# A hybrid GLA and Fourier layer on one core: folding the Fourier input before its projection instead of after it

## The chip, the core and the metric

The kernel runs on one core of one Trainium2 chip. Five engines work from queues of their own, each strictly in the order in which its instructions were written: TensorE (PE in the profile, with its weight loads shown apart as PEld), VectorE (DVE), ScalarE (ACT), GpSimd (POOL) and SyncE (SP), which issues the transfers between main memory and the on-chip memory. An instruction also waits for semaphores that other engines and landed transfers raise. The metric is the device time of one launch in microseconds (us), the median of several runs. Nothing is loaded ahead of the launch: all weights, some 360 MB of 32-bit floats, are read once in every run.

## What is computed

One layer of a backbone is applied to 128 context positions and 256 latent positions of width 2048 (384 rows in all). A modulated, normalised input `h` goes through one combined projection, whose last 1024 columns are four Fourier groups of 256 channels. The change is in this branch:

```python
proj = h @ lw['w_in']
q, k, v, g, lr_f, lr_b, fo = jnp.split(proj, splits, axis=-1)
...
fg = fo.astype(jnp.float32).reshape(bsz, t, FOURIER_GROUPS, FOURIER_GROUP_DIM)
f = jnp.fft.fft2(fg, axes=(1, 3), norm='ortho').real
f = f.reshape(bsz, t, FOURIER_WIDTH).astype(h.dtype)
gates = jax.nn.sigmoid(h @ lw['w_gate'] + lw['b_gate'])
g_a, g_b = jnp.split(gates, 2, axis=-1)
merged = g_a * (o @ lw['w_br_gla']) + g_b * (f @ lw['w_br_four'])
return merged @ lw['w_out'], s_f, s_b
```

The transform is taken over positions and over the channels of a group, apart for context (128 positions) and latent (256 positions). Only its real part is kept. The real part of such a product is cos times cos minus sin times sin; a cosine sum needs only the even part of its input (x[n] plus x[N-n]) and a sine sum only the odd part (x[n] minus x[N-n]). So half of the input, folded, is enough for each. Around this branch stand a gated linear attention (GLA) with two scans, a modulation computed from a large weight (`w_ada`), an output projection, and a feed-forward part that fills the second half of the run.

## The kernel before, in words

**Number format.** Each weight tile and each activation is split into a high part (the value rounded to the fast 32-bit matmul format, made by a ScalarE copy) and a low part (the rest, made by a VectorE subtraction). A product is the sum of three matmuls: high times high, high times low, low times high.

**The weight stream.** Weights come through one queue of tiles of 128 x 1024 floats (512 KB). `load()` (L193) issues the transfer of the next tile into one of two buffers named `raw`. `split()` (L214) makes its high part `whi` (L227) and its low part `wlo` (L228), four buffers each. `push()` is one load and one split; `take()` gives the oldest split tile to the matmuls; `grab()` (L248) does both. Three split tiles stand ready ahead of the one in use. A third tile's transfer can be issued only when the first tile's buffer has been read for the last time, which is its low-part subtraction.

**Stages.** After a head stage (up to some 130 us) come six q and k tiles and then 32 gate tiles (`proj`, L281), each of two weight tiles with 24 matmuls of 384 columns. During the gates a side generator advances the GLA by a step per weight tile, and a second generator, `ada_rest` (L589), advances the modulation: one step loads one more 512 KB tile `adaw` and runs two VectorE multiply-adds over 1024 elements (L600). `rate[0]` is the number of such steps per turn: 1.0 in the gates, 0.9 in the Fourier stage, 0 in the mixing stage, 0.82 in the output projection.

**The Fourier stage** (L991 to L1027). The 384 rows of `h` are the stationary operand and 512 columns of the weight the moving one: for each half of the channels, eight weight tiles of 18 matmuls (`products`, L266, called for the tile `pfo`). Then VectorE forms the channel sums and differences `ed` (L1009 to L1011). The generator `dft` transforms first over positions (`left`, L914, with tables `cd`) and then over channels (`turn_channels`, L950, with tables `cs2` and `odd`), in plain 32-bit matmuls (`pp`, `pn`, `pe`), into `eT` and `dT`. The channel N/2 (`nyq`) is handled apart. Half of this lies in the Fourier stage, half in the first steps of the next.

**The mixing stage** (L1083 to L1107). `mix_order` (L160) interleaves three kinds of work: 8 output gate tiles ("o": two weight tiles each, evicted by `gcol`), 16 Fourier branch tiles ("b", `four`, L1054; the weight is folded over its channels by `fold`, L204, into a tile `ws`), and 16 GLA branch tiles ("a"). Of the 16 "b", ten stand among the "o" and six among the "a".

The order on PE, DVE, ACT and POOL is exactly that of the program text. On SP the transfers are placed by the framework, near the place where they are called, and are issued in that order.

## Time and profile before

| what | value |
|---|---|
| median of 3 runs | 1953.94 us (1952.92 to 1954.0) |
| span of the profiled execution | 1950.6 us |
| PE busy | 1936.3 us (99%), 10422 matmul records |
| DVE busy | 1633.1 us (84%) |
| ACT busy | 906.9 us (46%) |
| DMA | 380.12 MB, mean 195 GB/s |
| chain that ended last | PE 96%, DVE 2%, DMA 2%, ACT 1% |

The span is the time from the first to the last instruction of one profiled execution. The median lies some 3.3 us above it, for what lies around the program. PE records overlap one another (the next matmul starts while the last drains), so the duration of one record is longer than the distance from one matmul to the next, and it is the distance that counts. A plain 32-bit matmul shows two records.

### The profile page before, as it was taken

The page shows a single profiled execution, that of the slowest core. Times are in us where ns is not written, and L with a number is a line of the kernel's source. Part 1 is how long each engine was busy: PE and PEld are TensorE (multiplying, and loading weights), DVE is VectorE, ACT ScalarE, POOL GpSimd, SP SyncE. Part 2 cuts the span into 40 slices and gives each one's busy share as a digit, 9 for nine tenths or more (in the row PEclk, how much of TensorE's full clock was granted, in tenths as well). Part 3 has the DMA queues.
Part 4 walks back from the last instruction along what each step waited for, and adds up shares of the span by engine and source line. Part 5 has one row for each costly group of instructions (what it writes and reads, how often), then busy time and mean ns, then how long its engine had stood idle before and what let it go on. Part 6 is the DMA issues. An engine that isn't in the chain of part 4 may idle for free.

```text
span 1950.6 us, 27243 instructions
## 1 busy us (share of the span) xinstructions
PE 1936.3 (99%) x10422; PEld 1705.2 (87%) x10422; DVE 1633.1 (84%) x2114; ACT 906.9 (46%) x1270; POOL 33.6 (2%) x55
## 2 busy tenths in 40 slices
PE   9999999999999999999999999999999999999998
PEld 5779999999889999999988888888888888888886
DVE  5668888878777797977789898999898999887876
ACT  4233554544336654446454444444444444444444
POOL 0000000000000000004000000000000000000001
PEclk9999999999999999999999999999999999999999
DMA  9978677767765786655355535463636263626244
GB/s 391 382 255 272 228 257 239 231 218 244 239 198 178 236 265 212 233 188 210 93 157 162 172 125 179 137 199 112 199 120 209 93 216 98 211 75 194 67 157 144
DMA packets 201179, 380.12 MB, mean 195 GB/s; under 512 B 14160, under 2 KB 127508, under 8 KB 196696
## 3 DMA queue, kind: packets, MB, share of 16 engines
q1 hardware_dynamic: 200520, 378.12, 58.4%
q8 instruction: 82, 1.34, 0.3%
q14 instruction: 49, 0.40, 0.1%
q10 hardware_dynamic: 528, 0.26, 0.0%
HBM read 361.55 MB, written 16.78 MB: 194 GB/s over the span
## 4 chain that ended last, share of the span: by engine, by line
PE 96%; DVE 2%; DMA 2%; ACT 1%; issue 0%; SPq 0%; POOL 0%; DVEq 0%; ACTq 0%; POOLq 0%
PE pmm L261 32%; PE pgu L273 30%; PE pdn L273 18%; PE pfo L273 3%; PE pv L415 3%; PE pgm L398 1%; PE pf L1064 1%; PE pmm L1320 1%; DMA slab<-in_w_ada 1%; PE ptr L1612 1%; PE pf L1065 1%; PE po L673 1%; DMA xraw<-in_w_x 0%; PE px L433 0%; DMA raw<-in_w_d 0%; DVE x1b L1764 0%
## 5 line engine op out<-in xcount | busy, mean ns | idle before, releaser
L261 PE MATMUL pmm<-A_hi,whi 128*128 128x384 f32 x1072 | 361.3, 337 | 0.0
L261 PE MATMUL pmm<-A_hi,wlo 128*128 128x384 f32 x1072 | 358.6, 335 | 0.0
L261 PE MATMUL pmm<-A_lo,whi 128*128 128x384 f32 x1072 | 358.5, 334 | 0.0
L1467 ACT CAST whi<-u 128x1024 fp32r<-128x1024 f32 x200 | 210.6, 1053 | 271.0 <-DVE u L1451 86.2
L227 ACT CAST whi<-raw 128x1024 fp32r<-128x1024 f32 x181 | 189.5, 1050 | 208.1 <-DMA raw<-in_w_gate 69.0
L1467 ACT CAST whi<-raw 128x1024 fp32r<-128x1024 f32 x175 | 184.2, 1053 | 212.1 <-DMA raw<-in_w_g 68.0
L228 DVE TENSOR_TENSOR wlo<-raw,whi 128x1024 fp32r<-128x1024 f32 x179 | 218.1, 1221 | 66.2 <-ACT whi L227 65.5
L1478 DVE TENSOR_TENSOR wlo<-u,whi 128x1024 fp32r<-128x1024 f32 x200 | 243.9, 1220 | 28.1 <-ACT whi L1467 16.9
L273 PE MATMUL pgu<-whi,A_hi 128*128 128x512 f32 x640 | 250.0, 391 | 0.0
L273 PE MATMUL pgu<-whi,A_lo 128*128 128x512 f32 x640 | 249.3, 389 | 0.0
L1478 DVE TENSOR_TENSOR wlo<-raw,whi 128x1024 fp32r<-128x1024 f32 x175 | 213.3, 1219 | 33.9 <-ACT whi L1467 24.6
L600 DVE SCALAR_TENSOR_TENSOR adacc<-adaw,spad,adacc 128x1024 f32<-128x1024 f32 x180 | 222.8, 1279 | 0.3
L261 PEld LDWEIGHTS pmm<-A_hi,whi 128*128 128x128 f32 x1072 | 201.2, 188 | 3.0 <-issue 1.4
L261 PEld LDWEIGHTS pmm<-A_lo,whi 128*128 128x128 f32 x1072 | 201.3, 188 | 0.3
L261 PEld LDWEIGHTS pmm<-A_hi,wlo 128*128 128x128 f32 x1072 | 201.2, 188 | 0.0
L273 PE MATMUL pdn<-whi,hid_hi 128*128 128x512 f32 x480 | 186.9, 389 | 0.0
L273 PE MATMUL pdn<-whi,hid_lo 128*128 128x512 f32 x480 | 186.8, 389 | 0.0
L273 PE MATMUL pgu<-wlo,A_hi 128*128 128x512 f32 x640 | 184.2, 389 | 0.0
L273 PEld LDWEIGHTS pgu<-whi,A_hi 128*128 128x128 f32 x640 | 120.1, 188 | 26.0 <-issue 0.8
L273 PEld LDWEIGHTS pgu<-wlo,A_hi 128*128 128x128 f32 x640 | 120.1, 188 | 25.4
L273 PEld LDWEIGHTS pgu<-whi,A_lo 128*128 128x128 f32 x640 | 120.1, 188 | 25.0
L273 PE MATMUL pgu<-whi,S 128*128 128x512 f32 x480 | 131.1, 395 | 0.0
(386 smaller groups left out, 2900.0 us busy)
## 6 DMA issues: line engine op xcount, KB each, us to landing
adaw<-in_w_ada SPq DMA_DIRECT2D x96, 512.0 KB, 4.1
raw<-in_w_d SPq DMA_DIRECT2D x88, 512.0 KB, 4.6
slab<-in_w_ada SPq DMA_DIRECT2D x32, 1024.0 KB, 10.4
raw<-in_w_gate SPq DMA_DIRECT2D x64, 512.0 KB, 4.7
raw<-in_w_g SPq DMA_DIRECT2D x48, 512.0 KB, 4.2
raw<-in_w_u SPq DMA_DIRECT2D x48, 512.0 KB, 3.8
raw<-in_w_in SPq DMA_DIRECT2D x44, 512.0 KB, 4.2
u<-in_w_u SPq DMA_DIRECT2D x40, 512.0 KB, 4.4
```

Source lines behind the costliest of these rows:

```text
L227: ACT.copy(hi, raw)
L228: sub = lambda: eng.tensor_sub(lo, raw, hi.bitcast(F32))
L261: PE.matmul(dst, w[wi][:, k * n + n0 : k * n + n0 + P], x[xi][:, k0 + k, :], start=first and k == 0 and j == 0, stop=last and k == kts - 1 ...
L273: PE.matmul(dst, stat[x_][m], mov(w[w_], m), start=first and w_ == m == x_ == 0, stop=last and w_ == m == 1,)
L398: PE.matmul(pgv[q : q + 32, :], spad[:, k, :], slab[k // (KT // 2)][:, k % (KT // 2), :], start=k < 4, stop=k >= KT - 4,)
L415: PE.matmul(pv[2 * t + g], hT[x_][:, kb, t * P : (t + 1) * P], w_[:, g * 512 : (g + 1) * 512], start=kb == 0 and j == 0, stop=kb == KT - 1 ...
L600: DVE.scalar_tensor_tensor(acc[:, c, :], w, spad[:, k, c : c + 1], acc[:, c, :], op0=ALU.mult, op1=ALU.add,)
L673: PE.matmul(dst, w[wi], x[xi], start=first and j == 0, stop=last and j == 2)
L1064: PE.matmul(pf[:, 0 : 2 * HT], w[0][:, c], x[k], start=k == 0, stop=False)
L1065: PE.matmul(pf[:, 0:HT], w[1][:, c], x[k][:, 0:HT], start=False, stop=m == 1 and k == 3)
L1467: ACT.copy(hi, src)
L1478: DVE.tensor_sub(lo, src, hi.bitcast(F32))
```

## The change

Both sides of the Fourier projection are folded before it.

- `h` is folded over positions: `over_ends` adds its high and low parts and forms x[n] + x[N-n] (65 and 129 columns, together `HT` = 194) and x[n] - x[N-n] (63 and 127, together 190); `over_parts` splits the result into `hF`, which holds 8 of the 16 depth tiles at a time. The first 8 are made at the end of the gates (generator `ahead`), the rest inside the Fourier loop.
- The weight is folded over channels in place in its `raw` buffer: `fold_across` does a VectorE subtraction and a multiply-subtract, each over 512 elements, and a small ScalarE copy of the channel N/2 into `wq`. For these tiles the low-part subtraction is not written right after the high-part copy; it is kept in `low_due` and written in the next `split()`, after that tile's `fold_across`.
- The weight is now the stationary operand. Only even-even (194 columns) and odd-odd (190 columns) products are formed: 24 matmuls per weight tile. The loop goes over depth outside and channel halves inside; all four groups gather in four banks at once, the channel N/2 in a fifth (`pfq`).
- The transform is taken over channels first (`turned`) and over positions second (`along`), wholly in the mixing stage. The tables are one transfer of 128 x 1934 floats (`cd`) in place of one of 128 x 646, four of 128 x 128 and four of one row.
- The modulation has no step in the Fourier stage (rate 0), 0.35 in the mixing stage, and 1.1 in the gates while the GLA runs. The GLA takes two steps at turns 41 and 49. In `mix_order` eight "b" stand among the "o" and eight among the "a".

The diff, cut to its core:

```diff
-    for h in range(2):
-        for n in range(8):
+    across = set()
+    for n in range(8):
+        for h in range(2):
             src = a["w_in"][16 + 4 * h : 20 + 4 * h, n // 4, :, 256 * (n % 4) : 256 * (n % 4) + 256]
+            across.add(len(srcs))
             srcs.append(src.rearrange("n p x -> p n x"))
...
-    mix_order = [("o", 0)]
-    for i in range(1, 8):
-        mix_order += [("o", i)] + [("b", next(fourier)) for _ in range(1 + (i in (1, 3, 5)))]
+    mix_order = [("o", 0), ("o", 1), ("o", 2)]
+    for i in range(3, 8):
+        mix_order += [("o", i)] + [("b", next(fourier)) for _ in range(1 + (i > 4))]
     for i in range(KT):
         mix_order.append(("a", i))
-        if i in range(1, 13, 2):
+        if i in range(1, 13) and i % 3:
             mix_order.append(("b", next(fourier)))
...
+    def fold_across(raw):
+        x, y = raw.rearrange("p (g i x) -> i p g x", g=2, i=2)
+        DVE.tensor_sub(y, x, y)
+        DVE.scalar_tensor_tensor(x, x, 2.0, y, op0=ALU.mult, op1=ALU.subtract)
+        n, h = divmod(next(crossed), 2)
+        ACT.copy(
+            wq[:, 2 * n : 2 * n + 2, 2 * h : 2 * h + 2],
+            raw.rearrange("p (g i k c) -> p i c k g", g=2, i=2, k=2)[:, 1, 0],
+        )
...
             raw, pairs = raws.pop(0)
+            if pairs == 2:
+                fold_across(raw)
+            while low_due:
+                low_due.pop()()
...
-            if pairs and hold:
+            if pairs == 2:
+                ACT.copy(hi, raw)
+                low_due.append(lambda: (DVE.tensor_sub(lo, raw, hi.bitcast(F32)), ready.append((hi, lo))))
+            elif pairs and hold:
                 half_done.append(rest)
...
+    def over_ends(k, t, r):
+        DVE.tensor_add(t, *(x[:, k : k + 2, :].bitcast(F32) for x in hT))
+        ACT.copy(r[:, :, 0 : HC + 1 : HC], t[:, :, 0 : TC + 1 : TC])
+        for lo, n, e in ((0, TC, 0), (TC, TL, HC)):
+            h, o = n // 2, HT + (0 if lo == 0 else HC - 2)
+            hi = lo + n - 1
+            DVE.tensor_add(r[:, :, e + 1 : e + 1 + h], t[:, :, lo + 1 : lo + 1 + h], t[:, :, hi : hi - h : -1])
+            DVE.tensor_sub(r[:, :, o : o + h - 1], t[:, :, lo + 1 : lo + h], t[:, :, hi : hi - h + 1 : -1])
+    def over_parts(k, r, x):
+        split_act(*(y[:, k % 8 : k % 8 + 2, :] for y in x), r)
...
         def side():
+            n = 0
             while True:
-                next(gl, None)
-                next(ada, None)
+                n += 1
+                more = [next(gl, 1) for _ in range(1 + (n in (41, 49)))]
+                if more[-1] is None or next(pre, 1) is not None:
+                    next(ada, None)
                 yield
-        rate[0] = 1.0
+        rate[0] = 1.1
...
+            def turned(h, m):
+                y = pc.tile([P, 2, 2, P], F32, tag="hr" if m else "ht", name="yq")
+                for n in range(2):
+                    lo, hi = rows_of(m, n)
+                    r_ = hi - lo
+                    pp = pss.tile([P, 2, 129], F32, tag="side", name="pp")
+                    for k in range(2):
+                        g = 2 * h + k
+                        if m == 0:
+                            PE.matmul(pp[0:r_, k, :], X[g][:, lo:hi], table(C_CE + 129 * g, 129), start=True, stop=False)
+                            PE.matmul(pp[0:r_, k, :], xq[:, lo:hi], table(C_OD + 129 * g, 129), start=False, stop=True)
+                        else:
+                            off = (P - 32 * g) % P
+                            PE.matmul(pp[0:r_, k, 0:P], X[g][:, lo:hi], table(C_CS + off, P), start=True, stop=True)
+                    ACT.copy(y[0:r_, n], pp[0:r_, :, 0:P])
...
+            def along(m, pe, stat):
+                PE.matmul(pe, stat(0, P), table(C_CT + at, HT), start=True, stop=False)
+                PE.matmul(pe[:, HC:HT], stat(1, r_), table(C_CT + at + HT, HL, r_), start=False, stop=True)
...
-        rate[0] = 0.9
-        for h in range(2):
-            p = [psm.tile([P, 512], F32, tag="mm", name="pfo") for _ in range(3)]
-            for n in range(8):
+        rate[0] = 0.0
+        xb = [pss.tile([P, T], F32, tag="side", name="pfo") for _ in range(4)]
+        qb = pss.tile([P, HT], F32, tag="side", name="pfq")
+        for n in range(8):
+            for h in range(2):
                 w = take()
-                if n < 7:
-                    push()
-                products(w, todo, by_tile=n in (0, 7))
+                push()
+                for w_ in range(2):
+                    for k in range(2):
+                        for x_ in range(2 - w_):
+                            mov = hF[x_][:, kt % 8, :]
+                            for g in range(2):
+                                for i, (lo, hi, _) in enumerate(parts):
+                                    PE.matmul(
+                                        xb[2 * h + g][:, lo:hi], four_w[w_][:, i, k, g, :], mov[:, lo:hi],
+                                        start=first and x_ == i == 0, stop=last and i == 1,
+                                    )
+                if h and n % 2:
...
+                            PE.matmul(
+                                qb[q : q + 4, :], wq[:, k, :], hF[x_][:, k % 8, 0:HT].bitcast(F32),
+                                start=k < 4 and x_ == 0, stop=k >= KT - 4 and x_ == 1,
+                            )
+                if 2 <= n < 6:
+                    if h == 0:
+                        over_ends(2 * n + 4, t, r)
+                    else:
+                        over_parts(2 * n + 4, r, hF)
...
-        rate[0] = 0.0
+        rate[0] = 0.35
         mT, late = None, []
         for b, i in mix_order:
...
             if b == "b":
+                for _ in df:
+                    pass
                 four(i)
```

More of the change, by code (lines that the diff above doesn't have):

```diff
@@ L199, in load @@
             SP.dma_start(dst, src)
-            raws.append((raw, n in folded))
+            raws.append((raw, 1 if n in folded else 2 if n in across else 0))
     fold_in = []
@@ L212, in tile_step @@
     half_done = []
+    low_due = []
+    crossed = iter(range(KT))
+    wq = const.tile([P, KT, 4], F32, name="wq")
+    def fold_across(raw):
[7 more added lines that the diff above has]
+        )
     def split(at=None, eng=DVE, hold=False, defer=None):
@@ L222, in split @@
             )
-            if pairs:
+            if pairs == 1:
                 raw = fold(raw)
@@ L924, in dft @@
             for h in range(2):
[L925 removed]
+                for m, dst in enumerate((eT, dT)):
+                    y = turned(h, m)
                     yield
[L927 to L943 removed]
@@ L944, in dft @@
-                turn_channels(*cols_of)
-                if h == 1:
-                    ACT.copy(pnr, nyqT)
-                    DVE.tensor_sub(pnr[64:96], nyqT[64:96], pnr[64:96].bitcast(F32))
-                yield
-        def turn_channels(g, x):
-            rot = cs2.rearrange("p m n c -> p m (n c)")
-            off = (P - 32 * g) % P
-            for m, dst in enumerate((eT[g], dT[g])):
-                pe = pss.tile([P, HT], F32, tag="side", name="pe")
-                PE.matmul(pe, rot[:, m, off : off + P], x[:, m], start=True, stop=m == 1)
-                if m == 0:
-                    PE.matmul(pe, odd[:, g, :], nyqT, start=False, stop=True)
-                split_act(dst[:, 0:HT], dst[:, HT:], pe)
+                    for k in range(2):
+                        pe = pss.tile([P, HT], F32, tag="side", name="pe")
+                        along(m, pe, lambda n, r_: y[0:r_, n, k, :])
+                        split_act(dst[2 * h + k][:, 0:HT], dst[2 * h + k][:, HT:], pe)
@@ L961, in nyq_weights @@
+                    if h == 1 and m == 0:
+                        pn = pss.tile([P, HT], F32, tag="side", name="pn")
+                        along(0, pn[0:96], lambda n, r_: nyq[0:r_, n, :])
+                        ACT.copy(pnr[0:96], pn[0:96])
+                        DVE.tensor_sub(pnr[64:96], pn[64:96], pnr[64:96].bitcast(F32))
         def nyq_weights():
@@ L1025, in tile_step @@
+        for q in range(0, P, 32):
+            ACT.copy(xq[q : q + 4, :], qb[q : q + 4, :])
+        for _ in nw:
+            pass
+        oT = alloc_r("B", "o")
         gates, raw_gates = {}, []
```

150 lines of the change are left out of this document (68 added, 82 removed).

## Prediction

> **What bounds the kernel now.** I read the page first (busy times and the chain by engine), then the chain in order of time around the change, then windows by stage.
>
> ```profile
> span 1950.6 us, 27243 instructions
> PE 1936.3 (99%) x10422; PEld 1705.2 (87%) x10422; DVE 1633.1 (84%) x2114; ACT 906.9 (46%) x1270; POOL 33.6 (2%) x55
> PE 96%; DVE 2%; DMA 2%; ACT 1%; issue 0%; SPq 0%; POOL 0%; DVEq 0%; ACTq 0%; POOLq 0%
> 484.40 12.51 PE pmm L261 x72
> 496.91 36.76 PE pfo L273 x162
> 547.25 20.45 PE pfo L273 x90
> 567.70 4.19 PE pmm L261 x24
> 180.00:497.00 317.00, 317.00 (x2049) 312.39 (x2048) 273.93 (x342) 151.35 (x253) 1.86 (x6) 1.00 0.73 240
> 497.00:535.00 38.00, 38.00 (x176) 31.68 (x175) 27.13 (x28) 12.61 (x19) 2.74 (x4) 1.00 0.70 229
> 535.00:570.00 35.00, 35.00 (x172) 29.94 (x171) 27.39 (x31) 11.23 (x22) 0.00 (x0) 1.00 0.70 222
> 680.00:745.00 65.00, 65.00 (x392) 65.00 (x391) 56.99 (x108) 34.40 (x59) 0.00 (x0) 1.00 0.83 269
> ```
>
> TensorE is on the chain nearly always, so a saved matmul is a gain as long as its weights arrive. In the window rows (length, then busy time of PE, PEld, DVE, ACT, POOL, clock, DMA) PE is full in every stage and the granted clock 1.00. The Fourier stage runs from 496.91 to 567.70: 70.8 us. Its 288 matmuls of 512 columns follow each other at 36.76/162 = 0.227 us, 65.4 in all; the other 5.4 us are the first half of the transform. The 384-column ones take 12.51/72 = 0.174.
>
> **The change part by part.**
>
> 1. The matmuls of the projection. 288 of 512 columns become 16 x 24 = 384 of 194 or 190 columns, each with a weight load of its own.
>
> ```profile
> 218.53 0.19 PEld L718 LDWEIGHTS bT<-cg,lah 128*128 128x128 f32 x1
> 218.64 0.19 PEld L718 LDWEIGHTS bT<-cg,lal 128*128 128x128 f32 x1
> 218.75 0.19 PEld L718 LDWEIGHTS bT<-cg,lah 128*128 128x128 f32 x1
> L398 PE MATMUL pgm<-slab,spad 128*32 128x256 f32 x512 | 31.5, 383 | 0.1
> ```
>
> By columns alone a 194-wide matmul would follow at about 0.09 us (0.227 - 318 x (0.227 - 0.174)/128 = 0.095), but behind one another weight loads start no closer than 0.11. I take 0.112: 2.7 us per weight tile, 43 us in all, 22 less than now (31 less at 0.09). The channel N/2 adds 32 plain 32-bit matmuls with 4 output columns, in four column places as in the L398 row, which takes 31.5/256 = 0.12 us each: 3 us, or 10 if four columns do not overlap. Were TensorE the bound, the stage would take 46 to 53 us.
>
> 2. The weight stream, which I hold for the new bound. In the built order VectorE's queue holds, for Fourier tile N: the two folding operations of tile N, then the low part of tile N-1. Tile N+1 loads into the buffer of tile N-1 and waits for that low part, so it waits for tile N to have landed and been folded. Before, the low part of tile N-1 waited for nothing of tile N, and two loads were under way at once; now only one is. The period of a tile is then a whole load, a fold and a low part in series.
>
> ```profile
> L199 SPq DMA_DIRECT2D raw<-in_w_in x19: 327/378/420, 482.5 to 561.8; - x19
> DMA to landing us min/median/max: 3.4/4.5/12.2
> 514.93 0.38 SPq L199 DMA_DIRECT2D raw<-in_w_in  x1
> 518.87 1.05 ACT L227 CAST whi<-raw 128x1024 fp32r<-128x1024 f32 x1 [1.72 <-DMA raw<-in_w_in]
> 534.26 0.39 SPq L199 DMA_DIRECT2D raw<-in_w_in  x1
> 538.29 1.06 ACT L227 CAST whi<-raw 128x1024 fp32r<-128x1024 f32 x1 [2.25 <-DMA raw<-in_w_in]
> L208 DVE TENSOR_TENSOR ws<-raw x16: 680/684/695, 576.2 to 721.5; 128x512 f32<-128x512 f32 x16
> L600 DVE SCALAR_TENSOR_TENSOR adacc<-adaw,spad,adacc 128x1024 f32<-128x1024 f32 x180 | 222.8, 1279 | 0.3
> L228 DVE TENSOR_TENSOR wlo<-raw,whi 128x1024 fp32r<-128x1024 f32 x179 | 218.1, 1221 | 66.2 <-ACT whi L227 65.5
> ```
>
> From issue to the first reader a load of this form took 538.29 - 534.26 = 4.03 with little beside it and 3.94 at 514.93; the shortest landing of any load was 3.4. The subtraction over 512 elements is 0.68; the multiply-subtract over 512 lies between that and 1.28 (the 1024-element row), and I take 0.70, since its length is that of the first; the low part is 1.22. With 0.1 for three hand-overs: 4.0 + 0.68 + 0.70 + 1.22 + 0.1 = 6.7 us per tile against TensorE's 2.7. With a 3.4 load it is 6.1. The folding over positions (four times one sum of 768 elements, four short ones and a low part, some 3.2 us) lies in the 4 us in which VectorE waits for the load, so I cost it at nothing; without that cover it costs 13.
>
> 3. The start of the stage. TensorE has three tiles ready at 496.9 and works to 505.0.
>
> ```profile
> 503.08 0.33 SPq L883 DMA_DIRECT2D cd<-in_consts  x1
> 508.39 0.42 SPq L199 DMA_DIRECT2D raw<-in_w_in  x1
> 512.60 1.05 ACT L227 CAST whi<-raw 128x1024 fp32r<-128x1024 f32 x1 [7.06 <-DMA raw<-in_w_in]
> 518.46 0.38 SPq L199 DMA_DIRECT2D raw<-in_w_in  x1
> 523.41 1.05 ACT L227 CAST whi<-raw 128x1024 fp32r<-128x1024 f32 x1 [2.53 <-DMA raw<-in_w_in]
> ```
>
> On SP, tile 4 still stands behind the tables, which wait for the last gate's store (503.08). Eight small table transfers are gone from between, the tables are three times as long. I issue it at 506 (503.9 if right behind, 508.39 as now). With 4.2 for the load (512.60 - 508.39) it is there at 510.2, folded and tile 3's low part done at 512.9. Tile 5 is followed by four gate loads and one `adaw`; I give it the 4.95 of 523.41 - 518.46, and tile 4 is ready at 512.9 + 4.95 + 2.7 = 520.6. Ten periods on, tile 14 is ready at 587.6, tile 15 some 1.3 later; two tiles of matmuls end at 593.0, the last eight of channel N/2 at 594.5. The first output-gate tile, loaded from 587.6, is split by 593.9. Stage end 594.5 against 567.7: **27 us later**.
>
> 4. The transform. It leaves the Fourier stage, and none of it lies beside other TensorE work.
>
> ```profile
> 533.51 1.50 PE L919 MATMUL pp<-cd,ed 128*128 128x65 f32 x12
> 534.85 0.83 PE L919 MATMUL pn<-cd,nyq 128*128 128x65 f32 x6
> 540.99 0.49 PE L956 MATMUL pe<-xa,cs 128*128 128x194 f32 x2
> 541.32 0.49 PE L958 MATMUL pe<-nyqT,odd 128*128 128x194 f32 x2
> ```
>
> Twelve records of `pp` take 534.85 - 533.51 = 1.34, two records of 194 columns 0.33. Now: 24 channel matmuls at 2 x 0.112 = 5.4, nine pairs over positions at 0.33 + 0.22 = 5.0, 10.4 in all. The half that stood in the mixing stage cost 5.4 (2 x 1.34 + 0.67 + 6 x 0.33). So the mixing stage gets **5 us** longer; the other half is counted in the 70.8.
>
> 5. VectorE in the mixing stage. About 10 modulation steps, 2 x 1.28 each, come in from the Fourier stage, and two "b" move among the "a".
>
> ```profile
> L1069 DVE TENSOR_TENSOR fd<-fd,pf 128x194 f32<-128x194 f32 x12 | 3.7, 349 | 0.0
> L1073 DVE TENSOR_TENSOR y<-fd 128x64 f32<-128x64 f32 (+1 forms) x12 | 3.1, 256 | 0.2
> L1074 DVE TENSOR_TENSOR y<-fd 128x64 f32<-128x64 f32 (+1 forms) x12 | 3.0, 252 | 0.0
> L1077 DVE TENSOR_TENSOR y<-y,gate 128x384 f32<-128x384 f32 x6 | 3.3, 558 | 0.2
> ```
>
> A "b" costs VectorE 2 x 0.68 + 1.22 + 2 x 0.35 + 4 x 0.25 + 0.56 = 4.9 and TensorE about 2.4. In the "a" window of 65 us VectorE would have 57.0 + 9.8 + 5 x 2.6 = 80 against TensorE's 70. Three tiles split ahead cover about 10 us of that lag. Between 0 and 10 I take **3**, as the cover is nearly the size of the excess. Among the "o" VectorE has room.
>
> 6. The gates. The number of modulation steps stays about the same there, the folding of eight depth tiles adds 4 x 3.2 = 13 us to VectorE's 274 of 317. Still 91%, so 0 to 5 us for stalls at the two double GLA steps; I take **1**. The removed VectorE sums `ed` and the POOL clearing of `odd` were covered by TensorE: nothing.
>
> Sum: 27 + 5 + 3 + 1 = 36, from the profiled 1950.6 to 1986.6, and with the 3.3 us by which the median exceeds that span, **1990 us**. The Trainium skill ("DMA: Bandwidth & Descriptors", section "Anatomy of one DMA", for the GpSimd path) fits a transfer as 2.0 us and its bytes at 436 GB/s, which is an estimate of 3.2 us for 512 KB. By that the period would be 5.9 and the sum 8 us lower; the rows here show 3.9 and more.
>
> **The rivals.**
>
> A. It is faster: tiles arrive as fast as now. Loads are issued 3.5 us apart at present (514.93, 518.46), and if the next load did not really wait behind the fold, the stage would be held by VectorE, 16 x 2.6 + 13 = 55 us against 70.8. That is -16 + 5 + 3 = -8, so 1946; with VectorE's part hidden as well, TensorE's 46 us, 1937. It decides for faster when the period of a tile falls below about 3.5 us, since ten periods must then end 32 us earlier. Against it is the queue order. Chance 0.12.
>
> B. TensorE's clock falls.
>
> ```profile
> 20.00:1949.00 1929.00, 1920.50 (x10337) 1695.18 (x10336) 1624.26 (x2091) 894.51 (x1246) 32.23 (x46) 1.00 0.58 193
> ```
>
> In each period TensorE would stand still for 6.7 - 2.7 = 4.0 us; now all its idle time from 20 us on sums to 1929.0 - 1920.5 = 8.5 us, and the clock is 1.00. At half speed a tile takes 5.4, which still fits into 6.7; the last two tiles, the eight small matmuls and the first output gates would lose 8 to 10 us: 1999. The Trainium skill ("TensorE: Matmul & The Clock Gate", "Part 1: The HAM clock gate") says that an idle window of about 3.4 us halves the clock; no run shown here has such gaps. It needs the series loads of step 2. Chance 0.15.
>
> C. VectorE's excess in the mixing stage is not covered, and the gates lose their 5: 10 + 5 in place of 3 + 1, 2001. For it: 80 against 70 in the "a" window, DMA share 0.83 there already. Against: the three tiles ahead. Chance 0.13.
>
> D. The loads are in series but shorter (3.4) and issued early at the start: 10 x 0.6 + 2 less, 1981; anything that hides a part of the chain puts it between 1955 and 1978. Chance 0.1 for the latter.
>
> **How the numbers follow.** Forecast (series loads, 1978 to 1998): 0.5; A 0.12, B 0.15, C 0.13, D's lower part 0.1. A measurement tells a change from none from about 0.2%, 4 us. Slower is all but A and the lowest end of D: 0.86; same 0.02; faster 0.12. The range 1966 to 2010 leaves out A and a little at each end.
>
> **What the changed profile would show.** Fourier weight loads about 6.7 us apart between 520 and 588; PE busy some 40% there, its idle time ended by the low part; VectorE waiting for the load at the first folding operation; 384 matmuls 0.11 us apart in bursts of 24; the first output-gate matmul near 594; VectorE above 95% among the "a". I am wrong if loads come at 4 us or closer, if TensorE's bursts take other than 2.7 us, or if the mixing stage grows by more than 15.

## The result, and the profile after

The changed kernel takes 2021.13 us (median of 4 runs, 2016.67 to 2022.91) against 1953.43 (4 runs, 1952.89 to 1954.0): 1.0343 times as long, 95% interval 1.0328 to 1.0357. It is 68 us slower where the forecast was 36. The direction was right, the size was not, and the time lies above the range. The profiled run took 2022.91, the slowest of the four.

Three lines of the page after: the span, the engines' busy time, the chain that ended last.

```profile
span 2021.1 us, 27652 instructions
PE 1954.2 (97%) x10582; PEld 1719.4 (85%) x10582; DVE 1673.4 (83%) x2184; ACT 913.2 (45%) x1292; POOL 33.2 (2%) x55
PE 72%; DVE 12%; DMA 10%; ACT 3%; issue 3%; SPq 0%; POOL 0%; ACTq 0%; DVEq 0%; POOLq 0%
```

TensorE held 96% of the chain; now 28% of it belongs to others, and VectorE has 40 us more work. Where the time came from is read from windows by stage, each from about the first matmul of a stage to the first of the next (within 1 us). First the kernel before: gates, Fourier stage, output gates with "b", GLA branch tiles with "b", output projection (columns as in the prediction: length, then busy time of PE, PEld, DVE, ACT, POOL, clock, DMA share, GB/s).

```profile
193.00:497.00 304.00, 304.00 (x1974) 299.39 (x1973) 261.01 (x331) 146.98 (x249) 1.86 (x6) 1.00 0.73 238
497.00:568.00 71.00, 71.00 (x333) 59.63 (x332) 53.12 (x55) 23.38 (x37) 2.74 (x4) 1.00 0.72 232
568.00:667.00 99.00, 99.00 (x623) 98.72 (x622) 73.65 (x134) 62.62 (x97) 0.00 (x0) 1.00 0.54 173
667.00:748.00 81.00, 81.00 (x487) 81.00 (x486) 68.76 (x129) 43.12 (x74) 0.00 (x0) 1.00 0.86 282
748.00:884.00 136.00, 136.00 (x807) 134.18 (x806) 111.61 (x138) 64.41 (x103) 0.00 (x0) 1.00 0.61 201
```

The same five stages of the changed kernel:

```profile
193.30:509.50 316.20, 306.42 (x1974) 299.67 (x1973) 270.61 (x351) 148.38 (x253) 1.87 (x6) 1.00 0.71 230
509.50:608.60 99.10, 69.81 (x449) 63.59 (x448) 60.57 (x83) 27.16 (x45) 2.31 (x4) 0.78 0.37 118
608.60:713.20 104.60, 102.52 (x632) 99.17 (x629) 72.72 (x120) 59.60 (x94) 0.00 (x0) 1.00 0.53 170
713.20:811.80 98.60, 90.06 (x522) 87.36 (x521) 91.49 (x165) 46.55 (x83) 0.00 (x0) 0.98 0.82 267
811.80:953.70 141.90, 139.46 (x807) 137.15 (x806) 114.29 (x141) 66.10 (x105) 0.00 (x0) 0.98 0.62 201
```

The five stages took 691.0 us and take 760.4. Their excesses are 12.2, 28.1, 5.6, 17.6 and 5.9 us; about 1 us more lies outside them. So only some 28 of the 70 us (of span) come from the stage that the change is about. TensorE was busy in every microsecond of these stages before and now stands still for 52 of them.

Inside the Fourier stage, VectorE's timeline over two tiles (start, duration, idle time before and what ended it) and, behind it, SyncE's:

```profile
535.36 0.69 DVE L232 TENSOR_TENSOR raw<-raw 128x512 f32<-128x512 f32 x1 [3.66 <-DMA raw<-in_w_in]
536.09 0.69 DVE L233 SCALAR_TENSOR_TENSOR raw<-raw 128x512 f32<-128x512 f32 x1
536.70 1.22 DVE L264 TENSOR_TENSOR wlo<-raw,whi 128x1024 fp32r<-128x1024 f32 x1
541.47 0.69 DVE L232 TENSOR_TENSOR raw<-raw 128x512 f32<-128x512 f32 x1 [3.56 <-DMA raw<-in_w_in]
...
542.81 1.22 DVE L264 TENSOR_TENSOR wlo<-raw,whi 128x1024 fp32r<-128x1024 f32 x1
547.44 0.69 DVE L232 TENSOR_TENSOR raw<-raw 128x512 f32<-128x512 f32 x1 [3.42 <-DMA raw<-in_w_in]
```

```profile
537.94 0.38 SPq L211 DMA_DIRECT2D raw<-in_w_in  x1
544.05 0.38 SPq L211 DMA_DIRECT2D raw<-in_w_in  x1
```

The fold of tile N (L232, L233) starts when its load lands, the low part of tile N-1 (L264) follows, and at its end (537.92, 544.03) the next load is issued. Fold to fold is 541.47 - 535.36 = 6.11 us, in it 541.47 - 537.94 = 3.53 of load.

The granted clock over three stretches of the same stage:

```profile
525.00:543.00 18.00, 12.89 (x88) 11.22 (x88) 6.62 (x10) 2.71 (x6) 0.00 (x0) 0.80 0.59 200
543.00:560.00 17.00, 14.78 (x75) 13.13 (x76) 9.23 (x14) 4.46 (x7) 0.00 (x0) 0.50 0.27 93
560.00:582.00 22.00, 13.79 (x88) 13.07 (x87) 14.92 (x23) 6.26 (x12) 0.00 (x0) 0.84 0.24 73
```

For 17 us TensorE ran at half speed, and looks busier there than beside it. In TensorE's timeline the same matmuls are seen at both speeds (a row can stand for several matmuls, the count stands at the end):

```profile
539.84 0.61 PE L1058 MATMUL pfo<-hF_hi,whi 128*128 128x194 f32 x4
540.29 0.61 PE L1058 MATMUL pfo<-hF_lo,whi 128*128 128x194 f32 x4
...
544.08 2.02 PE L1058 MATMUL pfo<-hF_hi,wlo 128*128 128x194 f32 x8 [3.19 <-DVE wlo L264]
545.90 1.05 PE L1058 MATMUL pfo<-hF_hi,whi 128*128 128x194 f32 x4
```

Four take 540.29 - 539.84 = 0.45 us before the wait of 3.19 us, eight take 545.90 - 544.08 = 1.82 after it: 0.11 each, then 0.23.

The start of the stage, on VectorE and on SyncE (the tables, then the load of the fifth weight tile, which is tile 4 counted from 0):

```profile
517.75 4.87 DVE L633 SCALAR_TENSOR_TENSOR adacc<-adaw,spad,adacc 128x1024 f32<-128x1024 f32 x4
```

```profile
522.41 0.33 SPq L945 DMA_DIRECT2D cd<-in_consts  x1
525.11 0.40 SPq L211 DMA_DIRECT2D raw<-in_w_in  x1
```

VectorE comes late into the stage: between the folds of the first tiles its queue holds the last part of the folding of `h` (until 515.37) and two modulation steps left over from the gates (the four multiply-adds above). So the low part of tile 2 ends at 525.08, and only then is the load of tile 4 issued. The tables wait for the store of the last gate, which ScalarE evicts some 8 us after TensorE has gone on to this stage (509.5), but they are issued ahead of that load and do not hold it.

### The profile page after: what moved, and what is told of

It is laid out like the page before. It is cut to its first block, busy times and chain, and to the rows that moved or that the text cites. A ratio compares the mean times of both kernels' runs of the same rounds, so it can differ in the third digit from the quotient of the medians.

```text
span 2021.1 us, 27652 instructions
## 1 busy us (share of the span) xinstructions
PE 1954.2 (97%) x10582; PEld 1719.4 (85%) x10582; DVE 1673.4 (83%) x2184; ACT 913.2 (45%) x1292; POOL 33.2 (2%) x55
## 4 chain that ended last, share of the span: by engine, by line
PE 72%; DVE 12%; DMA 10%; ACT 3%; issue 3%; SPq 0%; POOL 0%; ACTq 0%; DVEq 0%; POOLq 0%
PE pgu L306 29%; PE pdn L306 17%; PE pmm L294 17%; DVE adacc L633 4%; DMA raw<-in_w_in 3%; PE pv L448 3%; DVE wlo L258 2%; DMA raw<-in_w_br_gla 2%; ACT whi L257 1%; PE pgm L431 1%; DMA raw<-in_w_gate 1%; PE pmm L1385 1%; DVE wlo L264 1%; DMA adaw<-in_w_ada 1%; DMA slab<-in_w_ada 1%
## 5 line engine op out<-in xcount | busy, mean ns | idle before, releaser
L1532 ACT CAST whi<-raw 128x1024 fp32r<-128x1024 f32 x175 | 184.2, 1053 | 199.3 <-PE pgu L306 69.6
L257 ACT CAST whi<-raw 128x1024 fp32r<-128x1024 f32 x165 | 172.8, 1050 | 185.4 <-DMA raw<-in_w_gate 90.7
L258 DVE TENSOR_TENSOR wlo<-raw,whi 128x1024 fp32r<-128x1024 f32 x163 | 198.7, 1221 | 56.3 <-ACT whi L257 55.6
L1543 DVE TENSOR_TENSOR wlo<-raw,whi 128x1024 fp32r<-128x1024 f32 x175 | 213.5, 1220 | 36.5 <-ACT whi L1532 26.3
```

Of the source, the lines that this page charges most:

```text
L257: ACT.copy(hi, raw)
L258: sub = lambda: eng.tensor_sub(lo, raw, hi.bitcast(F32))
L1532: ACT.copy(hi, src)
L1543: DVE.tensor_sub(lo, src, hi.bitcast(F32))
```

## The experiments

Each ran once unless said otherwise; the kernel before took 1952.9 to 1954.1 beside them. Five questions: what holds the Fourier stage, whether the half clock costs anything, what the gates lost, what the mixing stage lost, and whether a kernel without these losses is faster than before. All edits are against the changed kernel unless another is named.

**1. Low part first.**

```diff
+            while low_due:
+                low_due.pop()()
             if pairs == 2:
                 fold_across(raw)
-            while low_due:
-                low_due.pop()()
```

> One edit to the changed kernel: the kept low part of tile N-1 is written ahead of the folding of tile N, not behind it, so that tile N-1's buffer comes free before tile N has landed. Theory (loads in series through the buffer): Fourier stage (first projection matmul to the first output-gate matmul) from 99 us to 64-76, loads about 4 us apart instead of 6.1, fewer half-clock stretches, total 2021 to 1980-1995. Rival (VectorE's own work in the stage is the bound, the order does not matter): stage stays above 92.

**2. A third load buffer, same order.** Every third Fourier tile loads into a buffer of its own (one `gate` buffer gives the room).

```diff
-                push()
+                load(pc.tile([P, G], F32, tag="raw3", name="raw") if (2 * n + h) % 3 == 2 else None)
+                split()
...
-                g = pc.tile([P, T], F32, tag="gate", name="gate", bufs=4)
+                g = pc.tile([P, T], F32, tag="gate", name="gate", bufs=3)
```

> The order of the changed kernel is kept (low part behind the next fold), but from Fourier tile 5 on the loads go round three buffers instead of two (the gate tiles of the mixing stage have three buffers in place of four, for room). Theory (loads in series through the buffer): the load of tile N+1 waits for the fold of tile N-1 only, so loads come 3.0-3.6 us apart, and the Fourier stage falls from 99 us to 66-78. Rival (it is the order itself, or VectorE's work): stage above 92.

Measured: 1999.2 us for the order and 1997.61 for the buffer; Fourier stage 81.5 and 78.2 us in place of 99.1. Three other kernels with an unaltered Fourier stage (experiments 3 and 4) have 96.2 to 101.0 there, so both gains are clear of the spread, but both stages end above the forecasts' upper ends (76 and 78). The row of the first folding operation, grouped over the stage (busy time and mean of one, then VectorE's idle time ahead of it), in the changed kernel, with the low part first, and with the buffer:

```profile
L232 DVE TENSOR_TENSOR raw<-raw 128x512 f32<-128x512 f32 x15 | 10.4, 691 | 28.6 <-DMA raw<-in_w_in 28.6
```

```profile
L232 DVE TENSOR_TENSOR raw<-raw 128x512 f32<-128x512 f32 x15 | 10.3, 685 | 3.4 <-DMA raw<-in_w_in 3.4
```

```profile
L232 DVE TENSOR_TENSOR raw<-raw 128x512 f32<-128x512 f32 x15 | 10.3, 685 | 8.0 <-DMA raw<-in_w_in 8.0
```

VectorE's wait for landings falls from 28.6 us to 3.4 and 8.0. Two unlike edits that share only the release of the buffer give the same, so the series of loads is shown to be the cause of some 18 to 21 us of the stage; the rest of its excess has other causes.

**3. The gates.** One edit lowers the rate of modulation steps from 1.1 to 1.0; the other also drops the two double GLA steps.

```diff
-        rate[0] = 1.1
+        rate[0] = 1.0
```

> One edit to the changed kernel: 1.0 modulation steps per turn in the gates instead of 1.1; about five steps more are left for the output projection. Theory (the denser steps put VectorE behind, and TensorE waits for GLA results): the gates (first to last gate matmul, 306 us against 295 before) take 295-298 and TensorE's idle time there falls from 9.8 to under 3; the output projection takes up to 8 more. Rival (the two double GLA steps and the folding over positions cost it): the gates stay above 303.

```diff
-                more = [next(gl, 1) for _ in range(1 + (n in (41, 49)))]
+                more = [next(gl, 1)]
...
-        rate[0] = 1.1
+        rate[0] = 1.0
```

> Two edits to the changed kernel, both in the gates: 1.0 modulation steps per turn instead of 1.1, and no double GLA steps at turns 41 and 49. In the run with 1.0 alone TensorE's only long wait there was 2.3 + 0.7 us at a cumulative-sum matmul of the GLA right at the second double step, with half-speed clock behind it. Theory (the double step puts a matmul behind its VectorE and ScalarE results in the same turn; the denser modulation makes the rest): the projection's first matmul at 497-499 us (503.1 with the double steps, 509.5 in the changed kernel, 496.7 before), TensorE idle under 1 us there, no half clock. Rival (folding over positions in the last turns costs it): first matmul after 502.

The window from the first gate to the first Fourier matmul, with the lower rate alone:

```profile
193.20:503.10 309.90, 306.95 (x1971) 301.96 (x1970) 263.31 (x342) 149.58 (x254) 1.86 (x6) 0.99 0.69 226
```

and without the double steps too:

```profile
193.20:497.20 304.00, 304.00 (x1974) 299.43 (x1973) 259.52 (x338) 147.55 (x252) 1.86 (x6) 1.00 0.71 232
```

The first takes 309.9 us in place of 316.2, the second 304.0, and then TensorE waits for nothing, as before the change. One run each has to be read with care here: four other kernels with unaltered gates (experiments 1, 2, 4 and 5) took 311.7 to 315.4. Both edits together therefore gain 8 to 12 us, clear of that spread; the lower rate alone gains 2 to 6, and it misses its forecast. The folding of `h` itself makes no wait here, but it is not free: only two of its four parts stand ahead of the first Fourier matmul in the second kernel (they start at 487.9 and 494.8, the others at 501.2 and 505.2), and with the rate back at 1.0 the gates hold three modulation steps fewer than before. What a double step does is seen in TensorE's timeline of the changed kernel (in brackets the wait and who ended it):

```profile
427.32 0.33 PE L766 MATMUL bT<-cg,lah 128*128 128x128 f32 x1 [2.28 <-ACT lah L335]
```

The next GLA step's matmuls stand on TensorE before its inputs are made. The same wait of 2.28 us stands in the traces of experiments 1 to 5 that have the double step, and in none without it. Neither edit makes the run shorter, 2028.89 and 2023.15 us: the steps not done in the gates come back in the output projection, 156.2 and 154.4 us against 141.9, where TensorE waits 11.0 and 7.1 us for modulation steps that are made in one piece.

**4. The mixing stage without modulation steps.**

```diff
-        rate[0] = 0.35
+        rate[0] = 0.0
```

> One edit to the changed kernel: no modulation steps in the mixing stage (0 instead of 0.35); the ten steps are left for the output projection. Theory (VectorE is over its share among the GLA branch tiles): that part falls from 98 us to 86-90 with TensorE's idle time under 3; the output projection, 142 us now, grows by 5 to 25. Rival (the two more Fourier branch tiles there, or the transfers, are the cause): the part stays above 95.

Windows of output gates, GLA branch and output projection:

```profile
605.90:708.50 102.60, 101.88 (x633) 99.19 (x630) 63.01 (x111) 59.99 (x95) 0.00 (x0) 1.00 0.46 146
708.50:796.20 87.70, 86.83 (x523) 85.99 (x522) 78.16 (x153) 47.75 (x86) 0.00 (x0) 1.00 0.84 283
796.20:963.00 166.80, 138.76 (x807) 135.31 (x805) 137.63 (x161) 64.49 (x103) 0.00 (x0) 0.92 0.62 197
```

The ten steps had cost 104.6 - 102.6 = 2.0 us among the output gates and 98.6 - 87.7 = 10.9 among the GLA branch tiles, whose time in the kernels with the rate of the change is 98.2 to 100.6. Among the output gates the spread (103.8 to 105.2) is nearly as large as the difference. The steps now cost 166.8 - 141.9 = 24.9 in the output projection, in one wait of TensorE of 25.9 us: steps left over near its end are made there in one piece (experiments 7 and 9). So VectorE's excess in the mixing stage is the ten steps, and moved in this way they cost more than they had. The run took 2032.6 us.

**5. The clock kept up.** Ten plain 128 x 128 matmuls of ones behind each Fourier tile's matmuls, on the kernel of experiment 1.

```diff
                                         start=first and x_ == i == 0, stop=last and i == 1,
                                     )
+                wt = psm.tile([P, P], F32, tag="mm", name="wt")
+                for _ in range(10):
+                    PE.matmul(wt, ones, ones, start=True, stop=True)
                 if h and n % 2:
```

> The edit of the first run (kept low part ahead of the next fold), and ten plain 128x128 matmuls of ones, into a bank that nothing reads, behind each Fourier tile's matmuls, some 2.2 us where TensorE otherwise waits. Theory (a part of the stage is TensorE at half clock, because it stands still between tiles): half clock in the stage falls from 31 us to under 8, matmuls stay 0.113 us apart, and the stage falls from 81.5 to 72-78 us though TensorE has 35 us more to do. Rival (the clock is hidden behind the loads and VectorE): the stage stays within 2 us of 81.5 or grows.

```profile
506.90:592.70 85.80, 82.95 (x770) 80.27 (x768) 61.05 (x83) 28.28 (x48) 2.31 (x4) 1.00 0.46 142
```

The clock is 1.00 and the stage 4.3 us longer, 85.8; the run 2004.99. But with the filler TensorE is busy for 82.95 of 85.8, so this dose is too large to price the half clock; experiment 8 has a smaller one.

**6. Repairs together.** The low part first, gates as in experiment 3's second kernel, a third buffer for some tiles, the tables issued in mid-stage, modulation steps at 0.6 among the output gates and none among the GLA branch tiles. A second kernel also moves the folding of h over positions from VectorE to POOL.

```diff
-        SP.dma_start(cd, a["consts"][:, C_CE:NC])
...
-                push()
+                load(pc.tile([P, G], F32, tag="raw3", name="raw") if 2 * n + h > 3 and (2 * n + h) % 3 == 1 else None)
+                split()
...
+                if h and n == 3:
+                    SP.dma_start(cd, a["consts"][:, C_CE:NC])
...
-        rate[0] = 0.35
+        rate[0] = 0.6
...
                     mT = alloc_A()
+                    rate[0] = 0.0
```

> A version meant to be better: low part ahead of the next fold; gates as before the change (1.0, no double steps); a third load buffer in part of the Fourier stage (three gate buffers in the mixing stage); the tables loaded in the middle of the stage and the weights of channel N/2 one turn pair later; 0.6 modulation steps per turn among the output gates and none among the GLA branch tiles. By the theory so far: gates end near 498, Fourier stage 62-70 (VectorE's 2.6 per tile and 3.2 per two tiles, and some half clock), mixing 188-194, output projection 136-140; total 1950-1966. If VectorE is not the next bound there, the stage would be under 58 and the total under 1946.

```diff
-        DVE.tensor_add(t, *(x[:, k : k + 2, :].bitcast(F32) for x in hT))
+        POOL.tensor_add(t, *(x[:, k : k + 2, :].bitcast(F32) for x in hT))
```

(and so for the other four sums of `over_ends`)

> The better version with the sums and differences over positions done by GpSimd instead of VectorE (384 elements took GpSimd 1.02 us before, VectorE 0.55). Theory (VectorE is the next bound of the Fourier stage): the stage falls by 5 to 12 us against the version with VectorE, total 1940-1958. Rival (GpSimd, some 5 us per pair of tiles, becomes the bound, or slows VectorE): the stage is as long or longer.

Both missed: 1997.62 and 2002.89 us. In the first: gates 305.8, Fourier 77.3, output gates 110.9, GLA branch 89.6, output projection 151.5. With the low part first VectorE waits in some tiles 1.17 us for the ScalarE copy of the tile that it folded last (4.6 us over the stage), and another 7.6 us for ScalarE's copies of the folded `h`. So the order cures the loads and leaves waits of another kind, as here on VectorE:

```profile
521.80 1.23 DVE L264 TENSOR_TENSOR wlo<-raw,whi 128x1024 fp32r<-128x1024 f32 x1 [1.17 <-ACT whi L263]
```

With POOL the Fourier stage is 84.9. The 768-element sum there and, in the changed kernel, on VectorE (grouped rows, busy time and mean ns of one):

```profile
L665 POOL TENSOR_TENSOR ht<-A_hi,A_lo 128x768 f32<-128x768 f32 x4 | 8.4, 2104 | 0.2
```

```profile
L665 DVE TENSOR_TENSOR ht<-A_hi,A_lo 128x768 f32<-128x768 f32 x4 | 3.8, 952 | 0.0
```

It takes 2.1 us in place of 0.95, in the chain that makes `hF`. VectorE gets slower too. This is its first folding operation in the kernel with POOL; without POOL its mean is 685 ns:

```profile
L232 DVE TENSOR_TENSOR raw<-raw 128x512 f32<-128x512 f32 x14 | 14.4, 1029 | 1.2 <-DMA raw<-in_w_in 1.2
```

So the rival's guess that POOL slows VectorE held.

**7. Repairs in the order of the change.** From the kernel of experiment 6: the fold before the low part again, the third buffer for every third tile, ScalarE's copy of `hF` a tile earlier, modulation steps 1.0 up to the first "b", then 0.3 up to the first "a", and 0.75 in the output projection.

```diff
                         over_ends(2 * n + 4, t, r)
+                        hk = [x[:, (2 * n + 4) % 8 : (2 * n + 4) % 8 + 2, :] for x in hF]
+                        ACT.copy(hk[0], r)
                     else:
-                        over_parts(2 * n + 4, r, hF)
+                        DVE.tensor_sub(hk[1], r, hk[0].bitcast(F32))
...
-        rate[0] = 0.6
+        rate[0] = 1.0
...
+                if mT is None:
+                    rate[0] = 0.3
                 four(i)
...
-        rate[0] = 0.82
+        rate[0] = 0.75
         spare_h
```

> A repaired kernel: a third buffer for every third weight tile of the Fourier stage (so that no load waits for the deferred low part), the tables issued in the middle of the stage, the ScalarE copy of each folded h a tile earlier, gates at rate 1.0 without double GLA steps, modulation steps among the first four output gates (1.0, then 0.3, none among the GLA branch tiles), 0.75 in the output projection. Theory V (once the loads are free, VectorE's work sets the time: 57 us in the Fourier stage): gates 304, Fourier stage 60 to 68, output gates about 107, GLA branch 86 to 88, output projection 137 to 140; run 1955 to 1968, no faster than before. Rival H (TensorE's half clock between bursts sets it): Fourier stage 75 or more with over 10 us lost to half clock; run above 1970. Rival T (TensorE is the bound once everything is repaired): Fourier stage 50 to 55, run 1940 to 1948.

Windows: the Fourier stage, the middle of it alone, then output gates, GLA branch, output projection.

```profile
497.70:565.80 68.10, 53.09 (x450) 48.85 (x448) 55.27 (x81) 26.31 (x44) 1.35 (x3) 0.87 0.48 151
527.00:561.00 34.00, 29.01 (x264) 26.91 (x263) 33.39 (x51) 14.50 (x26) 0.00 (x0) 1.00 0.47 145
565.80:675.50 109.70, 103.78 (x629) 99.32 (x630) 85.69 (x131) 60.59 (x96) 0.95 (x1) 1.00 0.58 185
675.50:766.70 91.20, 87.44 (x522) 85.86 (x521) 79.61 (x155) 48.24 (x85) 0.00 (x0) 1.00 0.81 268
766.70:920.20 153.50, 139.21 (x808) 135.84 (x806) 126.35 (x151) 64.39 (x104) 0.00 (x0) 0.94 0.63 200
```

Three successive folds in the middle of the stage:

```profile
539.56 0.69 DVE L232 TENSOR_TENSOR raw<-raw 128x512 f32<-128x512 f32 x1
...
542.89 0.68 DVE L232 TENSOR_TENSOR raw<-raw 128x512 f32<-128x512 f32 x1
...
547.42 0.69 DVE L232 TENSOR_TENSOR raw<-raw 128x512 f32<-128x512 f32 x1
```

Two tiles take 547.42 - 539.56 = 7.86 us, none of the folds waits, and VectorE is busy for 33.39 of 34.00 us: in the middle, with the loads free, it is the bound. The stage is 68.1 us, 2.7 shorter than in the kernel before. The run took 1988.68 us, above the 1955 to 1968 expected, and the largest part of the excess is the output projection. TensorE's timeline has its cause in the last of these rows; the first two are the entry of the Fourier stage:

```profile
512.30 2.02 PE L1058 MATMUL pfo<-hF_hi,wlo 128*128 128x194 f32 x8 [7.34 <-DVE wlo L264]
520.21 2.02 PE L1058 MATMUL pfo<-hF_hi,wlo 128*128 128x194 f32 x8 [2.47 <-DVE wlo L264]
...
890.39 1.85 PE L641 MATMUL pr<-adacc,selr 128*32 128x256 f32 x12 [13.69 <-DVE adacc L633]
```

Modulation steps left over at the fourth-last tile of the output projection are made there in one piece, and TensorE waits for them.

**8. The same with filler, and without the position fold.** Four filler matmuls per tile in place of experiment 5's ten; and the position fold inside the loop left out.

```diff
+                for _ in range(4):
+                    PE.matmul(wt, ones, ones, start=True, stop=True)
```

> The repaired kernel with four plain 128x128 matmuls of ones at the head of each of the 16 Fourier tiles (about 15 us of added TensorE work by the 36 us that ten per tile took), so that TensorE idles less and keeps its clock. Theory V: the Fourier stage stays within 3 us of the repaired kernel's, at a granted clock near 1.00. Rival H: it is 5 us or more shorter, since no work runs at half speed.

```diff
-                if 2 <= n < 6:
+                if 2 <= n < 2:
```

> The repaired kernel without the folding of h over positions inside the Fourier loop (the second eight depth tiles reuse the first eight's folded h, so this part of the computation is left out): 4 x 3.2 = 13 us less on VectorE, nothing else changed. Theory V: the Fourier stage is 10 to 13 us shorter than the repaired kernel's. Rivals H and T, or transfers as the bound: within 4 us of it.

The Fourier stage with filler, and without the fold:

```profile
498.90:571.10 72.20, 65.26 (x571) 62.13 (x569) 58.15 (x84) 29.50 (x49) 1.35 (x3) 0.91 0.48 150
```

```profile
497.60:559.10 61.50, 51.82 (x450) 48.58 (x448) 44.40 (x57) 22.64 (x36) 1.35 (x3) 0.86 0.51 169
```

The runs took 1991.29 and 1981.33 us. With filler the stage is 4.1 us longer, not shorter, and the clock rises only from 0.87 to 0.91, so the filler did not fully do what it was to, and neither theory's forecast came true. No gain from the clock was seen at either dose. Without the fold VectorE has 55.27 - 44.40 = 10.9 us less and the stage is 6.6 shorter: between the 10 to 13 of VectorE as the bound and the 4 of the rivals. VectorE sets the middle. The entry, where TensorE waits 7.34 and 2.47 us with this fold and 7.35 and 2.33 without it, is left as it was: in both kernels the folding of the first half of `h` is still in VectorE's queue there and ends at 509.8 in the kernel of experiment 7, and the next weight load is issued right behind it (509.92). No run moved that part away, so what the entry costs was not tested.

**9. The output projection at 0.95.** From the kernel of experiment 7; two runs.

```diff
-        rate[0] = 0.75
+        rate[0] = 0.95
```

> The repaired kernel with modulation steps at 0.95 in place of 0.75 in the output projection, so that all 21 fall due before the point at which the rest is drained at once (there TensorE waited 13.7 us for four of them). Theory Q (only the drain in one piece costs; spread out, they fit beside TensorE, VectorE's 126 us against 136): the wait at that point falls below 3 us and the output projection takes 137 to 143 us, run 1972 to 1977. Theory V (VectorE is short of time there too, so a step costs its 2.5 us wherever it stands): the stage stays at 148 or more, with TensorE waiting for low parts instead. By both it is slower than the kernel before.

```profile
879.27 0.64 PE L641 MATMUL pr<-adacc,selr 128*32 128x256 f32 x8 [1.58 <-DVE adacc L633]
```

The wait falls from 13.69 to 1.58 us and the stage from 153.5 to 143.9, a little over the 143 of theory Q: making them in one piece was most of the cost. 1976.72 us, 1.0117 times the kernel before (1.0084 to 1.0151). This is the fastest version found, 44 us below the changed kernel, and still slower than the kernel before. By its profiled run (span 1977.6 against 1950.6): gates 304.0 and Fourier 67.9 us, so 0 and -2.9; output gates 110.4, GLA branch 91.0, output projection 143.9, so +11.6, +9.8 and +7.8.

## Why the prediction was wrong in size

By its steps, as excesses of the profiled run over the one before. The sum had 27 for the Fourier stage, 8 for the mixing stage, 1 for the gates and nothing for the output projection; measured are 28.1, 23.2, 12.2 and 5.9. So the bound of the Fourier stage was found, and the step that failed is the assumption that VectorE's additional work in the other stages stays covered (steps 5 and 6).

- **Steps 2 and 3, the serial loads: the mechanism right, +27 forecast, +28 measured, and that the sizes agree so well is luck.** The queue order did what was read from it; experiments 1 and 2 show it. The period is 6.1 us, not 6.7, where the load took 3.5 (rival D's 3.4 was the better choice). From the fold of tile 5 (535.36) to that of tile 15 (598.25) ten periods took 62.9 us in place of 67, which gives back 4. The start lost about as much again. TensorE did not have three tiles ready, because VectorE came late into the stage: its first wait (3.5 us, for the low part of tile 1) ends at 517.9. The load of tile 4 was issued 15.6 us after the first Fourier matmul, where I had allowed 9.1, and what it waited for was the low part of tile 2, not the tables. Two misses cancelled.
- **Step 1, the matmuls: right.** They follow each other about 0.11 us apart at full clock and twice that at half; TensorE was not the bound of the Fourier stage in any version without filler.
- **Step 6, the gates: one term that failed, 1 forecast, 12.2 measured (8 to 12 over the five runs with these gates).** I looked for the cost in the folding of h, which makes no wait there (second kernel of experiment 3). It was the rate and the double steps, which make room for that folding: TensorE has GLA matmuls in its queue whose inputs come from VectorE and ScalarE, and VectorE's mean share (86% before and after, not the 91% of the prediction) hides that it is late at some of them. Taking them out moves the cost: 12 us less in the gates, 12.5 more in the output projection.
- **Step 5, VectorE in the mixing stage: the other term that failed, 3 forecast, 13 measured for the ten steps.** I set 80 us of VectorE work against 70 of TensorE and let three tiles of lead absorb the difference. The work was forecast well: 68.8 before, and with 9.8 and 13 more 91.6, where 91.5 were measured. But the window is 98.6 us long, longer than the work of either engine: TensorE waited 8.5 us in it and VectorE 7.1, so the two wait for each other and the lead did not cover it. The prediction's own sign of being wrong, a mixing stage that grows by more than 15, came true: it grew by 23.2.
- **The output projection: no term, 5.9 measured.** It carries 16 modulation steps as before. It starts with waits for the last merged tiles, 2.4 us together, and then loses 3.4 to half clock (granted clock 0.83 from 815 to 835). I read this as the lead that the stage before had used up; no run tests that alone, and in experiments 1, 2 and 5, which have the same mixing stage, the output projection takes 137.3 to 140.3 us, so only 1 to 4 more than before. The longer wait:

```profile
823.35 0.69 PE L294 MATMUL pmm<-A_lo,whi 128*128 128x384 f32 x1 [1.93 <-DVE A_lo L336]
```

- **Step 4, the transform: 5 forecast, 7.8 measured.** Added up from the start of each of its matmuls (`pp`, `pn`, `pe`) to the start of the next, it takes 12.7 us in the mixing stage, where 10.4 were forecast, and the half that stood there before took 5.0. Without modulation steps (experiment 4) output gates and GLA branch together are 190.3 us against 180.0, and TensorE waits for 1.6 of them, so the transform and these waits make up most of the 10.3.
- **Rivals as alternatives.** B (the clock) and C (the mixing stage and the gates) were given chances of their own, each as a case instead of the forecast. Both came about together with it: C's premises do not exclude the forecast's, and neither do B's. C's price, 15 for mixing stage and gates together, was too low too: 25. B's condition was met (granted clock 0.50 for 17 us), and its price was not found: with more of the clock granted the stage got no shorter (experiments 5 and 8), though the filler takes TensorE time itself, so 8 to 10 us at the end of the stage are not excluded. The Trainium skill ("TensorE: Matmul & The Clock Gate", "Part 1: The HAM clock gate") has an idle window of about 3.4 us halve the clock. Here such a window was not idle throughout: TensorE was busy for 1.33 of the 3.40 us from 529.10 to 532.50, and from 532.60 its clock is 0.50.
- **Rival A** (faster) had the right next bound, VectorE, and about the right amount of its work: 55 us forecast, 55.27 in experiment 7. But a stage is not as long as its busiest engine's work: it took 78 to 82 us without serial loads and 68.1 in experiment 7, where TensorE still waits at the entry. The saved time is then spent on the modulation steps that the Fourier stage used to carry.
- **Two slips of 1 us** change nothing: 32 matmuls of 0.12 us (step 1) are 4 us, not 3, and rival D's 1981 is 1982 by its own terms.

## What to carry to other kernels

A change that takes matmuls from TensorE and pays in VectorE work is to be costed over all the stages that share VectorE: here some 22 us of projection matmuls were saved (by the prediction's count) and 40 us of VectorE work added where VectorE was already busy for 568 of 691 us, and side work pushed out of one stage found no free place in the others. When an operation is deferred in an engine's queue, ask which buffer it still holds: here one late subtraction per tile put all loads in series. Alternatives that do not exclude one another are added, not chosen between.

## What the runs showed of the hardware

- TensorE's half clock came in some of the stretches between bursts that were 6 us apart (granted clock 0.80 from 525 to 543, 0.50 from 543 to 560, 0.84 from 560 to 582) and was gone where VectorE fed it a tile every 3.9 us (1.00 from 527 to 561 in experiment 7). In the Fourier stage of the changed kernel each halving followed 3.4 us in which TensorE was busy for 0.2 to 1.9.
- The sum over 768 elements takes 0.95 us on VectorE and 2.1 on POOL, and beside POOL's work VectorE's subtraction over 512 elements took 1.03 us in the mean in place of 0.69. That made an offload to the idle engine a loss.
- The multiply-subtract over 512 elements takes the same 0.69 us as the subtraction.
